# A Hymba layer on one core: weights of the heads, the GLU and the output projection split by two DMAs of GpSimd's queue

## The chip, the cores and the metric

The kernel runs on one core of a Trainium2 chip. The metric is the device time of one execution in microseconds; the time of a kernel is the median of its runs. The core has five engines that each run their own list of instructions in a fixed order: TensorE (PE), VectorE (DVE), ScalarE (ACT), GpSimd (POOL) and SyncE (SP, which here only issues DMAs). They wait for each other by semaphores.

## The reference

One layer of a hybrid decoder for one sequence of 1024 positions, width 1024, all in float32. Cut to what matters:

```
h = rms(x, norm1_w) * (1 + sc1) + sh1
u, q, k, v = split(h @ w_in, [512, 1024, 1152])        # "heads": q, k, v
y_ssm  = s5(u, ...)                                     # scan over positions, then
         # z = gelu(y);  out = z * sigmoid(z @ w_glu + b_glu)
y_attn = window_attention(rms(q), rms(k), v, rel_bias, sinks)   # window of 128
x = x + g1 * (concat(rms(y_ssm), rms(y_attn)) @ w_out)
h2 = rms(x, norm2_w) * (1 + sc2) + sh2
x = x + g2 * conv_ffn(h2, w_up, conv_w, conv_b, w_down)         # d_ff = 2816
```

sh1, sc1, g1, sh2, sc2, g2 come from `silu(c) @ w_mod + b_mod`.

## The kernel before

The kernel keeps the products near float32 by splitting each operand into two arrays of the type fp32r, a rounded half hi and the rest lo = array - hi. `mm3` (L143 to L147) then makes one product of three matmuls, hi by hi, hi by lo and lo by hi. So each weight has to be there twice before its lo can be used. `split` (L137 to L141) makes the pair from an array that stands in SBUF: ScalarE casts it into hi (L133), and VectorE, or GpSimd where the caller says so, subtracts hi from it into lo (L118).

The stages, with their place in the profiled execution:

- up to 128 us: modulation, first norm, operands of the S5 scan and its convolutions; the first two heads begin.
- 128 to 224 us: the six heads t0 to t5 (v, k and four pairs of q). `head_w` (L459) brings the weights of one head, 128 by 1024: a DMA of SyncE into the staging tile W0 (L461), a split into U0/U1 for even t and U2/U3 for odd t, and sixteen small matmuls that make a bias row. One head is 48 matmuls of 512 columns. VectorE does the scan, the norms of q and k and their splits beside it.
- 224 to 324 us: GELU (L725), the GLU and the first units of attention. The GLU weights go through W0 as two arrays and are split in four halves of 512 columns into HA and HB (L748 to L754). Attention runs in 16 units: ScalarE makes the exponentials (L835, L837), and a multiplication by the reciprocal of the sum (the rule PM picks GpSimd for it in all but two units) precedes PE's transposes and the product with v.
- 324 to 401 us: the rest of attention and the S5 half of the output projection. Its weights come in four arrays through W0 into HA and HB in turn (L897 to L901). VectorE makes the later modulation values from arrays that SyncE loads into S16 (`emit_mod`, L178).
- 401 to 477 us: the attention half of the output projection. `wload` (L869) brings eight arrays through W0 (W1 and W0 in turn for the last four) into pairs of U tiles.
- 477 us to the end: the conv FFN, up and down. Its weights have splits of their own that the change doesn't touch.

The order of the instructions on each engine is set ahead of the run: a scheduler with a simulated time line (L1358) gives each engine one list, and a tile name such as W0 or U0 is a slot whose next user waits until the last reader of the one before is done. A DMA that waits for its slot stands at the head of its engine's list, and what is behind it on that engine waits too. Before the change GpSimd issues no DMA in these stages; its list there holds only the multiplications of attention.

Of the kernel before, what the change touches and what calls it, by code (L numbers as in the profile page):

```python
# [9 lines left out]
F32 = mybir.dt.float32  # L10
# [4 lines left out]
ADD, SUB, MUL, MAX, MIN = ALU.add, ALU.subtract, ALU.mult, ALU.max, ALU.min  # L15
# [47 lines left out]
def hymba_kernel(ctx, tc, xT, c, wmod, wu, wkvq, small, consts, relb, pq, wglu, wout, wup, wdn, out):  # L63
# [7 lines left out]
    def new(tag, dt=F32):  # L71
        return pool.tile([128, SIZES.get(tag, 1024)], dt, tag=tag, name="t" + tag)
# [11 lines left out]
    def newr(tag):  # L84
        return RT(new(tag, F32R))

    vec, act, pol, sync = nc.vector, nc.scalar, nc.gpsimd, nc.sync
# [29 lines left out]
    def tt(eng, o, a, b, op):  # L117
        return eng.tensor_tensor(out=o, in0=a, in1=b, op=op)  # L118
# [12 lines left out]
    def cpy(e, o, i):  # L131
        if e == "a":
            act.copy(o, i)  # L133
        else:
            ENG[e].tensor_copy(out=o, in_=i)

    def split(x, src, hi_eng="a", lo_eng="v"):  # L137

        hi, lo = x
        cpy(hi_eng, hi.r, src)  # L140
        tt(ENG[lo_eng], lo.r, src, hi.f, SUB)  # L141

    def mm3(o, a, b, start, stop, chain=False):  # L143

        pe.matmul(o, a[0].r, b[0].r, start=start, stop=False, skip_group_check=chain)
        pe.matmul(o, a[0].r, b[1].r, start=False, stop=False, skip_group_check=chain)
        pe.matmul(o, a[1].r, b[0].r, start=False, stop=stop, skip_group_check=chain)  # L147
# [81 lines left out]
    for k in range(8):  # L229
        if k < 2:  # L230
            t_ = newr(("HA", "HB")[k])
# [6 lines left out]
    wst = None  # L238
    for k in range(8):
# [3 lines left out]
        if k % 2 == 0:  # L243
            wst = new(("W0", "A10")[k // 2 % 2])
            sync.dma_start(out=wst, in_=wu[k // 2])
        w = half(newr(f"U{k}") if k < 4 else wux[:, (k - 4) * 1024:(k - 3) * 1024])
# [27 lines left out]
    U = new("S16")[:, 0:4096]  # L274
# [182 lines left out]
    brow = pool.tile([2, 128 * 2], F32, name="brow")  # L457

    def head_w(t):  # L459
        wst = new("W0")  # L460
        sync.dma_start(out=wst, in_=wkvq[t])  # L461
        w = (newr(f"U{2 * (t % 2)}"), newr(f"U{2 * (t % 2) + 1}"))
        split(w, wst)
        if t >= 2:
            qn.append(new(("W1", "U4", "U5")[t - 2]) if t < 5 else qx)
        b, b2, r = abank(), abank(), brow[:, (t % 2) * 128:(t % 2 + 1) * 128]
        for k in range(8):
            ks = slice(k * 128, k * 128 + 128)
            pe.matmul(b[0:2, 0:128], shs[:, 2 * k:2 * k + 2], w[0].r[:, ks], start=(k == 0), stop=False)
            pe.matmul(b[0:2, 0:128], shs[:, 2 * k:2 * k + 2], w[1].r[:, ks], start=False, stop=(k == 7))  # L470
        vec.tensor_copy(out=r, in_=b[0:2, 0:128])
        with pe.pin(False):
            pe.matmul(b2[:, 0:1], r, ones[0:2, 0:1], start=True, stop=True)
        vec.tensor_copy(out=bcol[:, t:t + 1], in_=b2[:, 0:1])
        return w
# [145 lines left out]
    for q in range(4):  # L621
        sync.dma_start(out=kd[:, 8 * q:8 * q + 8, 112:240],
                       in_=ka[32 * q:32 * q + 16, :].rearrange("p (g x) -> p g x", x=128))
# [60 lines left out]
    for h in range(2):  # L684
        for i in range(4):
            q_ = newr(f"H{8 + 4 * h + i}")
            for kv in range(2):
# [3 lines left out]
                src = qn[i][p0, h * 512:h * 512 + 512]  # L691
# [23 lines left out]
    for i in range(8):  # L715
        b = bank[int(pick("YB", i))]
        for q in range(4):
            g = 4 * i + q
            o = b[:, q * 128:(q + 1) * 128]
            st = (SI if g % 2 else SR)[:, g // 2, 0:128]  # L720
# [7 lines left out]
    for m in range(4):  # L728
        zv = zT[m].rearrange("p (c t) -> p t c", t=8)
        for q2 in range(2):  # L730
            b = sbank()
            for q in range(4):
                t_ = 4 * q2 + q
# [13 lines left out]
    wg = []  # L747
    wgt = (newr("HA"), newr("HB"))  # L748
    for k in range(4):
        if k % 2 == 0:  # L750
            wst = new("W0")
            sync.dma_start(out=wst, in_=wglu[k // 2])
        wg.append(half(wgt[k // 2][:, (k % 2) * 1024:(k % 2 + 1) * 1024]))
        split(wg[k], wst[:, (k % 2) * 512:(k % 2) * 512 + 512])  # L754
    mx = {}
    bw = pool.tile([128, 8], F32, name="bw")
    ts(bw[:, 0:4], S("ons"), -0.5, MUL)
# [5 lines left out]
    for h in range(2):  # L763
# [9 lines left out]
        for n in range(4):  # L773
            src = zT[n][:, hs]
# [6 lines left out]
        for n in range(4):  # L781
            src = zT[n][:, hs]
# [27 lines left out]
    for n in range(8):  # L810
        av = bank[2]
        for kv in range(2):
# [6 lines left out]
            for i2 in range(2):  # L819
# [6 lines left out]
                for i1 in range(2):  # L826
                    i = 2 * i2 + i1
                    vec.tensor_tensor_reduce(  # L828
                        out=P[:, i, :], in0=b[:, i1 * 256:i1 * 256 + w_], in1=Tb[kv][:, i, 256 - w_:256],
# [31 lines left out]
    x = [xq[:, k * 1024:(k + 1) * 1024] for k in range(4)] + [new(f"X{k}") for k in range(4, 8)]  # L861
# [1 line left out]
        sync.dma_start(out=x[k], in_=xT[k])  # L863
    ld = [0]

    slots = [("U0", "U1"), ("U4", "U5"), ("U0", "U1")]
    slots += [(("U4", "U5"), ("U2", "U3"), ("U0", "U1"))[i % 3] for i in range(5)]

    def wload(src):  # L869
        i = ld[0]  # L870
        ld[0] += 1
        st = new("W0" if i < 4 else f"W{i % 2}")
        sync.dma_start(out=(st if len(src.shape) == 2 else st.rearrange("p (d c) -> p d c", d=2)), in_=src)
        w = (newr(slots[i][0]), newr(slots[i][1]))
        split(w, st)
        return w

    n2s = pool.tile([128, 8], F32, name="n2s")
# [1 line left out]
    wo2 = wout.rearrange("d p (b c) -> b p d c", b=2)  # L880
# [13 lines left out]
    wS = {}  # L894
    for i, d in enumerate(order):
        if i % 2 == 0:
            st = new("W0")  # L897
            sync.dma_start(out=st.rearrange("p (d c) -> p d c", d=2), in_=wo2[0, :, d:d + 2])
            t_ = newr(("HA", "HB")[(i // 2 + 1) % 2])
            w = (t_[:, 0:1024], t_[:, 1024:2048])  # L900
            split(w, st)  # L901
        wS[d] = w
        for h in range(2 if d > 3 else 1):
            proj(d, h, 0, bank[5 + h], w)
        for q in (2 * i, 2 * i + 1):
            with tc.issue_after(unit[MOD_AT[q]]):
                emit_mod(24 + q, mst[q % 3], cact3)
# [202 lines left out]
    G, W = {}, {}  # L1110
# [110 lines left out]
    for s_, (c_, i, p) in enumerate(steps):  # L1221
# [10 lines left out]
        if s_ in XP:  # L1232
            k = XP[s_]
# [128 lines left out]
```

## Time and profile before

| | us |
|---|---|
| median of 3 runs | 1139.48 |
| lowest and highest | 1139.41, 1142.07 |
| the profiled execution, its own time | 1142.15 |
| span of its trace | 1140.3 |

The own time of the profiled execution is 1.85 us longer than the span that the trace covers, from the first to the last instruction, and 2.67 us longer than the median of the runs. The mean clock that TensorE was granted is 0.958 of full speed. Engines are read by their busy time in a stage; what sets the end of a stage is read from the chain of waits, which follows the last instruction back to whatever released it.

### The profile page before, as it was taken

What the parts mean: (1) busy time and instruction counts of PE and PEld (TensorE: products, weight loads), DVE (VectorE), ACT (ScalarE), POOL (GpSimd) and SP (SyncE); (2) the same over time, 40 slices, a digit from 0 to 9 for tenths busy, and PEclk for the clock granted to TensorE, in tenths of its full rate; (3) what the DMA queues carried; (4) which work ended last, traced back from release to release, by engine and by line L of the source; (5) the groups of instructions that cost most, each with busy time, mean ns of one, the idle gap of its engine ahead of it and who ended that gap; (6) DMA issues with size and microseconds to landing.
All of it is one profiled execution on the core that took longest, in us unless ns stands there. A gap on an engine that the chain in (4) does not pass through costs nothing.

```text
span 1140.3 us, 13281 instructions
## 1 busy us (share of the span) xinstructions
PE 1053.4 (92%) x4692; PEld 828.2 (73%) x4692; DVE 957.5 (84%) x1541; ACT 550.2 (48%) x936; POOL 256.7 (23%) x137
## 2 busy tenths in 40 slices
PE   6979999688989899779999999999999989989998
PEld 4868777475646577657888888888888768768876
DVE  8996899969988988888777878797777787997985
ACT  5412443583874346745554545455444554434342
POOL 0000000002121001762122223212212142353541
PEclk9979999679989899989999999999999989999999
DMA  9501516025024743222223232423123359120002
GB/s 371 214 19 39 127 40 93 1 88 190 19 94 183 240 147 112 93 92 93 93 78 113 87 130 93 151 90 112 56 93 126 115 217 384 63 93 1 1 37 111
DMA packets 47333, 128.13 MB, mean 112 GB/s; under 512 B 6017, under 2 KB 13985, under 8 KB 47266
## 3 DMA queue, kind: packets, MB, share of 16 engines
q1 hardware_dynamic: 47266, 127.28, 32.8%
q8 instruction: 37, 0.61, 0.2%
q14 instruction: 30, 0.25, 0.1%
HBM read 105.28 MB, written 21.99 MB: 112 GB/s over the span
## 4 chain that ended last, share of the span: by engine, by line
PE 60%; DVE 29%; ACT 4%; DMA 3%; issue 3%; POOL 1%; SPq 0%; ACTq 0%; DVEq 0%; POOLq 0%
PE bk L97 54%; PE bk L99 6%; DVE tA L118 5%; DVE tU L118 3%; DVE tH L118 3%; DVE tS L118 2%; DVE tX L127 2%; DMA tW<-in_dram 2%; DVE bk L118 2%; DVE tS L180 1%; DVE tXQ L118 1%; DVE tXQ L127 1%; DVE tX L118 1%; DVE tX L180 1%; ACT tU L133 1%
## 5 line engine op out<-in xcount | busy, mean ns | idle before, releaser
L97 PE MATMUL bk<-tU,tU 128*128 128x512 f32 x516 | 124.9, 395 | 4.8 <-DVE tXQ L127 2.4
L97 PE MATMUL bk<-tA,tU 128*128 128x512 f32 x516 | 128.1, 395 | 0.8 <-DVE tA L118 0.8
L97 PEld LDWEIGHTS bk<-tU,tU 128*128 128x128 f32 x516 | 97.6, 190 | 27.8 <-issue 2.8
L97 PE MATMUL bk<-tH,tU 128*128 128x512 f32 x477 | 116.0, 392 | 0.0
L97 PEld LDWEIGHTS bk<-tA,tU 128*128 128x128 f32 x516 | 96.7, 188 | 24.2 <-DVE tA L118 1.4
L127 DVE SCALAR_TENSOR_TENSOR tX<-tH,sm,tX 128x1023 f32<-128x1023 f32 x66 | 100.5, 1523 | 8.0 <-ACT tX L1097 7.9
L97 PEld LDWEIGHTS bk<-tH,tU 128*128 128x128 f32 x477 | 89.1, 188 | 19.3
L97 PE MATMUL bk<-tA,tXQ 128*128 128x512 f32 x300 | 76.0, 401 | 2.1 <-ACT tH L1050 2.1
L118 POOL TENSOR_TENSOR tU<-tW,tU 128x512 fp32r<-128x512 f32 x25 | 36.3, 1462 | 174.1 <-ACT tU L133 152.4
L97 PE MATMUL bk<-tH,tA 128*128 128x512 f32 (+1 forms) x168 | 63.9, 509 | 11.4 <-ACT tH L133 7.6
L133 ACT CAST tU<-tW 128x512 fp32r<-128x512 f32 (+1 forms) x67 | 47.1, 710 | 48.9 <-PE bk L97 18.2
L97 PEld LDWEIGHTS bk<-tA,tXQ 128*128 128x128 f32 x300 | 57.4, 191 | 16.0 <-ACT tH L1050 2.5
L99 PE MATMUL bk<-tH,tU 128*128 128x512 f32 x267 | 64.0, 395 | 1.8 <-DVE tU L118 1.7
L118 POOL TENSOR_TENSOR tH<-tH,att 128x1024 f32<-128x1024 f32 (+1 forms) x9 | 19.1, 2124 | 195.8 <-DVE att L840 161.7
L118 DVE TENSOR_TENSOR tX<-tX,tX 128x512 f32<-128x512 f32 (+1 forms) x63 | 61.6, 981 | 0.8
L118 POOL TENSOR_TENSOR tXQ<-tW,tXQ 128x512 fp32r<-128x512 f32 x12 | 49.1, 4102 | 53.1 <-ACT tXQ L133 37.8
L99 PEld LDWEIGHTS bk<-tH,tU 128*128 128x128 f32 x267 | 49.6, 189 | 15.6 <-DVE tU L118 2.7
L97 PE MATMUL bk<-tXQ,tH 128*128 128x256 f32 (+2 forms) x224 | 51.9, 374 | 4.3 <-DVE att L828 4.3
L118 DVE TENSOR_TENSOR tU<-tW,tU 128x512 fp32r<-128x512 f32 (+2 forms) x43 | 37.8, 881 | 20.4 <-ACT tU L133 20.4
L97 PEld LDWEIGHTS bk<-tXQ,tH 128*128 128x128 f32 x224 | 45.1, 268 | 13.3 <-DVE att L828 9.0
L118 POOL TENSOR_TENSOR tU<-tX,tU 128x512 fp32r<-128x512 f32 x19 | 33.2, 1747 | 84.9 <-ACT tU L133 70.8
L118 DVE TENSOR_TENSOR tU<-tX,tU 128x512 fp32r<-128x512 f32 x39 | 31.3, 808 | 23.6 <-ACT tU L133 23.6
(349 smaller groups left out, 2398.9 us busy)
## 6 DMA issues: line engine op xcount, KB each, us to landing
tX<-in_dram SPq DMA_DIRECT2D x51, 512.0 KB, 3.3
tW<-in_dram SPq DMA_DIRECT2D x49, 512.0 KB, 3.3
tS<-in_dram SPq DMA_DIRECT2D x30, 512.0 KB, 6.0
gd<-tX SPq DMA_DIRECT2D x22, 512.0 KB, 2.9
tA<-in_dram SPq DMA_DIRECT2D x12, 512.0 KB, 9.7
tH<-in_dram SPq DMA_DIRECT2D x12, 512.0 KB, 4.2
tH<-gd SPq DMA_DIRECT2D x8, 512.0 KB, 4.7
tA<-gd SPq DMA_DIRECT2D x8, 512.0 KB, 8.9
```

Source lines behind the costliest of these rows:

```text
L97: return f(*a, **k)
L99: i = f(*a, **k)
L118: return eng.tensor_tensor(out=o, in0=a, in1=b, op=op)
L127: return vec.scalar_tensor_tensor(out=o, in0=a, scalar=s, in1=b, op0=op0, op1=op1)
L133: act.copy(o, i)
L180: vec.tensor_tensor_reduce(out=st, in0=st, in1=ca, scale=1.0, scalar=S("b_mod", j, 1), op0=MUL, op1=ADD, accum_out=mod[:, j:j + 1],)
```

## The change

A new helper `dsplit` takes the place of a staging load and a `split` where weights of the heads, the GLU and both halves of the output projection are brought in, 22 times in all. It issues a DMA on GpSimd's queue that reads the array from HBM and casts it into hi. ScalarE multiplies hi by -1 into lo. A second DMA on GpSimd's queue reads the array from HBM again and adds it onto lo. The staging tile W0 falls away there, and so do 20 loads on SyncE's queue and 22 subtractions on VectorE; 22 casts on ScalarE become 22 multiplications of the same width. GpSimd issues 44 DMAs that it did not issue before, 36 of 512 KB and 8 of 256 KB. The eight pairs of `wload` get other slots, among them W0/W1 for the third.

```diff
--- before.py
+++ after.py
@@ -139,6 +139,13 @@
         hi, lo = x
         cpy(hi_eng, hi.r, src)
         tt(ENG[lo_eng], lo.r, src, hi.f, SUB)
+
+    def dsplit(x, src, shape=None):
+
+        v = [(t_.r if shape is None else shape(t_.r)) for t_ in x]
+        pol.dma_start(out=v[0], in_=src)
+        act.mul(v[1], v[0].bitcast(F32), -1.0)
+        pol.dma_start(out=v[1], in_=src, accum_op=ADD)
 
     def mm3(o, a, b, start, stop, chain=False):
 
@@ -457,10 +464,8 @@
     brow = pool.tile([2, 128 * 2], F32, name="brow")
 
     def head_w(t):
-        wst = new("W0")
-        sync.dma_start(out=wst, in_=wkvq[t])
         w = (newr(f"U{2 * (t % 2)}"), newr(f"U{2 * (t % 2) + 1}"))
-        split(w, wst)
+        dsplit(w, wkvq[t])
         if t >= 2:
             qn.append(new(("W1", "U4", "U5")[t - 2]) if t < 5 else qx)
         b, b2, r = abank(), abank(), brow[:, (t % 2) * 128:(t % 2 + 1) * 128]
@@ -747,11 +752,8 @@
     wg = []
     wgt = (newr("HA"), newr("HB"))
     for k in range(4):
-        if k % 2 == 0:
-            wst = new("W0")
-            sync.dma_start(out=wst, in_=wglu[k // 2])
         wg.append(half(wgt[k // 2][:, (k % 2) * 1024:(k % 2 + 1) * 1024]))
-        split(wg[k], wst[:, (k % 2) * 512:(k % 2) * 512 + 512])
+        dsplit(wg[k], wglu[k // 2][:, (k % 2) * 512:(k % 2) * 512 + 512])
     mx = {}
     bw = pool.tile([128, 8], F32, name="bw")
     ts(bw[:, 0:4], S("ons"), -0.5, MUL)
@@ -863,16 +865,16 @@
         sync.dma_start(out=x[k], in_=xT[k])
     ld = [0]
 
-    slots = [("U0", "U1"), ("U4", "U5"), ("U0", "U1")]
-    slots += [(("U4", "U5"), ("U2", "U3"), ("U0", "U1"))[i % 3] for i in range(5)]
+    slots = [(f"U{i}", f"U{i + 1}") if i < 6 else ("W0", "W1") for i in (0, 4, 6, 2, 0, 4, 2, 4)]
+
+    def pairs(t_):
+        return t_.rearrange("p (d c) -> p d c", d=2)
 
     def wload(src):
         i = ld[0]
         ld[0] += 1
-        st = new("W0" if i < 4 else f"W{i % 2}")
-        sync.dma_start(out=(st if len(src.shape) == 2 else st.rearrange("p (d c) -> p d c", d=2)), in_=src)
         w = (newr(slots[i][0]), newr(slots[i][1]))
-        split(w, st)
+        dsplit(w, src, pairs)
         return w
 
     n2s = pool.tile([128, 8], F32, name="n2s")
@@ -894,11 +896,9 @@
     wS = {}
     for i, d in enumerate(order):
         if i % 2 == 0:
-            st = new("W0")
-            sync.dma_start(out=st.rearrange("p (d c) -> p d c", d=2), in_=wo2[0, :, d:d + 2])
             t_ = newr(("HA", "HB")[(i // 2 + 1) % 2])
             w = (t_[:, 0:1024], t_[:, 1024:2048])
-            split(w, st)
+            dsplit(w, wo2[0, :, d:d + 2], pairs)
         wS[d] = w
         for h in range(2 if d > 3 else 1):
             proj(d, h, 0, bank[5 + h], w)
```

The new order on each engine differs from the old one at the following places.

PE where head t1's first half ends and t2 begins (tHA, tHB, tH: the activations' halves; tU0/tU1: hi and lo of t2's weights; shs: the shift that makes the bias row). Before:

```order
L97 MATMUL bk0_63<-tH14_97,tU3_978 128x512
L97 MATMUL bk2_65<-tHA_85,tU0_1064 128x512 x2
L97 MATMUL bk3_66<-tHA_85,tU0_1064 128x512
L97 MATMUL bk6_69<-tX4_601,cn_73 128x512
L97 MATMUL bk3_66<-tHA_85,tU0_1064 128x512
L97 MATMUL bk2_65<-tHA_85,tU1_1065 128x512
L97 MATMUL bk5_68<-cn_73,brow_609 128x1
```

And after, on the same engine at the same place:

```order
L97 MATMUL bk0_63<-tH14_97,tU3_975 128x512
L97 MATMUL bk5_68<-cn_73,brow_609 128x1
L97 MATMUL bk6_69<-tX4_601,cn_73 128x512
L97 MATMUL bk2_65<-tHA_85,tU0_1060 128x512 x2
L97 MATMUL bk3_66<-tHA_85,tU0_1060 128x512 x2
L97 MATMUL bk5_68<-tU0_1060,shs_458 2x128
L97 MATMUL bk5_68<-tU1_1061,shs_458 2x128
```

In both, four matmuls of t2 can run on hi alone; what needs lo comes right behind them, and in the new order that is the bias row.

ACT at the end of the GELUs (the table loads switch ScalarE's function; L725 is the GELU, L835 and L837 the exponentials of attention). Before:

```order
L725 ACTIVATE tX7_1632<-bk6_69 128x4x8x16
L835 ACT_TABLE_LOAD
L835 ACTIVATE att_1992<-att_1992 128x4
L837 ACTIVATE tH4_1993,att_1992<-tH4_1993,att_1992 128x128 x4
L835 ACTIVATE att_1992<-att_1992 128x4
L837 ACTIVATE tH5_2023,att_1992<-tH5_2023,att_1992 128x128 x4
L133 CAST tHB_1797<-tW0_1804 128x512
L725 ACT_TABLE_LOAD
L725 ACTIVATE tX7_1632<-bk5_68 128x4x8x16
L133 CAST tHB_1797<-tW0_1804 128x512
L835 ACT_TABLE_LOAD
```

And after, where the GELU has L730 and the exponentials L837 and L839, and L147 is the negation in `dsplit`:

```order
L147 ACTIVATE tHA_1790<-tHA_1790 128x512
L730 ACTIVATE tX6_1625<-bk6_69 128x4x8x16
L730 ACTIVATE tX7_1626<-bk5_68 128x4x8x16
L730 ACTIVATE tX7_1626<-bk6_69 128x4x8x16
L837 ACT_TABLE_LOAD
L837 ACTIVATE att_1986<-att_1986 128x4
L839 ACTIVATE tH4_1987,att_1986<-tH4_1987,att_1986 128x128 x4
```

The last GELU now stands ahead of the exponentials, and one switch back and forth, two table loads, is gone.

POOL in the second half of attention (TENSOR_TENSOR: a unit's multiplication; L146 the casting DMA, L148 the adding one; tHA: weights of the S5 half of the output projection, tU: of the attention half). Before:

```order
L118 TENSOR_TENSOR tH_2381<-tH_2381,att 128x1024
L118 TENSOR_TENSOR tA_2417<-tA_2417,att 128x1024
L118 TENSOR_TENSOR tH_2491<-tH_2491,att 128x1024
L118 TENSOR_TENSOR tA_2529<-tA_2529,att 128x1024
L118 TENSOR_TENSOR tH_2565<-tH_2565,att 128x1024
```

And after, from the DMAs ahead of the multiplication that was the third of these:

```order
L146 DMA tU_2924<-in_dram 128x2x512
L146 DMA tHA<-in_dram 128x2x512
L118 TENSOR_TENSOR tH_2485<-tH_2485,att 128x1024
L148 DMA tU_2925<-in_dram 128x2x512
L148 DMA tHA<-in_dram 128x2x512
L118 TENSOR_TENSOR tA_2523<-tA_2523,att 128x1024
L146 DMA tU_3111<-in_dram 128x2x512
L118 TENSOR_TENSOR tH_2559<-tH_2559,att 128x1024
```

Each of the last three multiplications now has DMAs ahead of it that wait for a slot or for ScalarE's negation.

## Rows read from the trace of the kernel before

**Rows 1.** The page, its line of engines: busy time, share, instructions.
```profile
PE 1053.4 (92%) x4692; PEld 828.2 (73%) x4692; DVE 957.5 (84%) x1541; ACT 550.2 (48%) x936; POOL 256.7 (23%) x137
```

**Rows 2.** Busy time by stage: stretch, length, engines, clock, DMA share, GB/s.
```profile
128.00:224.00 96.00, 82.46 (x435) 61.55 (x423) 92.74 (x182) 41.74 (x63) 0.00 (x0) 0.92 0.32 64
256.00:324.00 68.00, 57.47 (x256) 38.37 (x256) 62.55 (x161) 44.55 (x114) 15.78 (x8) 0.93 0.29 99
324.00:369.00 45.00, 44.72 (x187) 28.28 (x186) 38.12 (x93) 24.26 (x70) 9.37 (x4) 0.95 0.46 163
369.00:401.00 32.00, 26.61 (x99) 17.16 (x98) 29.27 (x50) 11.26 (x17) 2.76 (x1) 0.89 0.70 229
515.00:1140.00 625.00, 605.15 (x2585) 488.56 (x2583) 509.37 (x607) 292.84 (x449) 180.51 (x106) 0.99 0.29 106
```

**Rows 3.** Chain of waits, 105 to 324 us: start, length, what.
```profile
105.53 17.63 PE bk L99 x181
...
138.13 1.13 DVE tU L118
...
173.64 1.22 DVE tU L118
...
201.69 0.70 DVE tU L118
...
245.05 1.28 ACT L725
...
247.47 1.28 ACT L835
...
308.36 1.14 DVE tHB L118
...
309.53 3.37 DMA tW<-in_dram
```

**Rows 4.** Chain of waits, 374 to 436 us.
```profile
374.42 1.15 DVE tHA L118
375.58 4.67 DMA tW<-in_dram
...
382.61 5.38 DMA tW<-in_dram
...
389.09 1.23 DVE tU L118
...
401.77 34.13 PE bk L99 x146
```

**Rows 5.** Time line of ACT in the heads: start, length, instruction, idle before it.
```profile
89.30 1.05 ACT L133 CAST tU<-tW 128x1024 fp32r<-128x1024 f32 x1
...
140.30 0.62 ACT L504 CAST tXQ<-tX 64x512 fp32r<-64x512 f32 x1
```

**Rows 6.** Time line of PE in the heads, and at the end of attention.
```profile
93.96 1.12 PE L99 MATMUL bk<-tU,shs 128*2 128x128 f32 x16
...
130.37 4.26 PE L99 MATMUL bk<-tH,tU 128*128 128x512 f32 x18
...
142.09 1.03 PE L97 MATMUL bk<-tHA,tU 128*128 128x512 f32 x2
...
195.15 3.26 PE L97 MATMUL bk<-tH,tU 128*128 128x512 f32 x13
...
387.79 2.95 PE L97 MATMUL bk<-tA,tHA 128*128 128x512 f32 x12
395.98 4.85 PE L97 MATMUL bk<-tA,tHA 128*128 128x512 f32 x12 [5.24 <-DVE tXQ L127]
```

**Rows 7.** DMA issues, whole span, then 360 to 400 us: KB, median us to landing.
```profile
tW<-in_dram SPq DMA_DIRECT2D x49, 512.0 KB, 3.3
...
tW<-in_dram SPq DMA_DIRECT2D x4, 512.0 KB, 4.7
```

**Rows 8.** POOL: the time line at 469 us, and line L118 by tile (ns).
```profile
469.29 31.15 POOL L118 TENSOR_TENSOR tXQ<-tW,tXQ 128x512 fp32r<-128x512 f32 x1 [5.30 <-ACT tXQ L133]
...
L118 POOL TENSOR_TENSOR tH<-tH,att x9: 1039/2161/2902, 243.5 to 370.6; 128x1024 f32<-128x1024 f32 x7, 128x512 f32<-128x512 f32 x2
```

## The prediction

> **What bounds the kernel now.** I read the busy times first. PE is busy for 92% of the span and DVE for 84%, GpSimd for 23% [rows 1], so time can only be won where PE waits. The busy times by stage say where that is. From 515 us on, PE is busy 605 of 625 us; the change edits nothing there, and I count it as zero. From 324 to 369 us PE is busy 44.72 of 45.00. From 128 to 224 us DVE is the fuller engine, 92.74 of 96 against PE's 82.46, and from 369 to 401 us PE has only 26.61 of 32 while DVE has 29.27 [rows 2]. The chain of waits was read next, for the pieces that belong to the weights. In the heads four of DVE's subtractions lie on it, 138.13 the first and 173.64 the last, of 1.10 to 1.22 us each, 4.57 together. Around 245 us two of ScalarE's table loads are on it, 1.28 each, and at 308 us one subtraction with the staging load behind it, 1.14 and 3.37 [rows 3]. From 374.42 to 390.32 us the chain is nothing but the staging tile W0 going round: subtract, load (4.67), cast, subtract, load (5.38), cast, subtract (1.23) [rows 4]. PE runs out of work behind it: it is idle for 5.24 us before 395.98, and the next 12 matmuls take 4.85 us where the 12 before took 2.95 [rows 6]. PE's busy rows from 401.77 on (34.13 us in one piece, rows 4) show it full again.
>
> **What a new pair costs.** Call D the time from the slot's release to the landing of lo. It holds a casting load, a negation and an adding load. No row shows a DMA that GpSimd issues, nor one that casts or adds. The nearest is SyncE's staging load of the same 512 KB, 3.3 us to landing at the median and 4.7 where the queue is busy [rows 7]. The negation is as wide as the cast that it replaces, 1.05 us [rows 5]. From below D is 3.3 + 1.05 + 3.3 = 7.65 us. From above I let the adding load cost two, since it also reads its destination, at the busy price: 4.7 + 1.05 + 9.4 = 15.2 us. I take 9.5, nearer the lower end, because the bytes and the array are those of the staging load; of it some 3.9 is the casting load, and about 4.5 is left for the adding one. Before, the staging tile hid the load, and cast and subtraction took only 1.05 + 1.22 after the slot was free. So a pair whose slot is freed late now comes later by about 7 us, and one whose slot is free early costs nothing on the path.
>
> **Heads: plus 4 us.** t0: ScalarE wrote the first half of the pair at 89.30 [rows 5], so the slot was free then; lo lands at 89.3 + 9.5 = 98.8. PE takes it for the bias row at 93.96 [rows 6]. That is 4.8 us of waiting, 3.0 to 10.5 by the bounds, on an engine on which the chain lies here (17.63 us in one piece from 105.53, rows 3); some 0.8 of it lies where PE waited for the bias row anyway, so plus 4. t1 is wanted only behind t0's last matmuls, at 134.6, and costs nothing. t2: its slot is freed when t0's last matmuls end, 130.37 + 4.26 = 134.6. The casting load lands at 138.5, but ScalarE is in its casts of k until 140.30 + 0.62 = 140.9, so the negation ends at 142.0 and lo lands at 146.5. PE arrives at 142.09 and can run four matmuls on hi, to 143.0: a wait of 3.5 us (0 to 9). t3 to t5 are freed early enough at a D of 9.5. DVE in turn loses its four subtractions, minus 4.57 on the chain. Both can't be had: PE's last head matmuls end at 195.15 + 3.26 = 198.4 [rows 6] and DVE takes their result at 201.69 [rows 3], 3.3 us later. With PE 3.5 later that margin is used up, and DVE, 4.57 faster, waits for PE. I count zero for this second step (from -4.6 to +5), and +4 for the heads.
>
> **GELU and GLU: minus 2 us.** The last GELU moves ahead of the exponentials, so that one switch back and forth falls away, 2 x 1.28 = 2.56 us [rows 3]. The first exponentials start later by about one GELU, which takes back some of it. The GLU weights are wanted only after the first units of attention. Bounds -2.6 and 0.
>
> **First half of the output projection, 256 to 324 us: minus 2 us.** Gone from the chain are 1.14 and 3.37 at 308.36 [rows 3]; that is 4.5, and DVE, 62.55 of 68 us busy [rows 2], stays next. But GpSimd's list now has the four DMAs of two pairs ahead of the multiplication of a unit. That one takes 2.16 us [rows 8] and used to start as soon as DVE was done; now it can wait for a slot and for ScalarE. I take half back. Bounds -4 and +3.
>
> **End of attention, 369 to 401 us: minus 6 us.** W0 no longer goes round: the first pairs of the attention half have slots of their own, the third (W0/W1) is loaded long before. Also three subtractions leave DVE. The most that PE can win is its idle 5.24 and the 1.9 by which 4.85 exceeds 2.95, 7.1 together [rows 6]. What is late next is DVE's modulation work, which fills the 29.27 us; less three subtractions it is 25.6, under PE's 26.6. Against it: the last three multiplications of attention stand behind DMAs, and PE has no slack from 324 to 369 us. I take 6, bounds -7 and 0.
>
> **Nothing for the rest.** The later pairs of `wload` (401 to 477 us) are hidden beside a full PE; uncovered, each would cost up to D less its lead. SyncE's 20 loads less win nothing, no chain piece waits for its issue. The second reading of some 10 MB lies beside a DMA share of at most 0.70 [rows 2], and is a part of D's upper bound.
>
> **Sum.** +4 - 2 - 2 - 6 = -6 us. The profiled execution took 1142.15 us (its span 1140.3 and 1.85 around it), so it would take 1136.15. That execution lay 2.67 us over the median of the runs, 1139.48, and the changed kernel is compared with that: 1139.48 - 6 = 1133.5 us. A difference under 0.3%, 3.4 us, can't be told from no change here.
>
> **Rivals.** *First, slower: GpSimd writes its DMAs late.* A GpSimd subtraction took 31.15 us at 469.29, where the larger multiplications of attention take 2.2 at the median, while DVE ran one subtraction after the other [rows 8]; GpSimd got nowhere until DVE let go. In the heads DVE is as full (92.74 of 96). If that, or a slow adding load, brings D to 15, t0 costs 9.7 instead of 4 and t2's wait grows to 9, of which 5.7 shows beyond the margin; t4 and t5, which would now come late too, add 2 more by my estimate; attention gives back the 2 at 256 us and half of the 6. That is 9.7 + 5.7 + 2 - 2 + 0 - 3 = +12.4, so 1152 us. It decides from a D of about 12, where t0 and t2 have eaten the 6 us. Against it: in the heads DVE does short operations with gaps, and the row stands alone: the longest of the nine multiplications in attention took 2.9 us, beside a DVE that was busy for 62.55 of 68 us [rows 2, 8].
>
> The Trainium skill ("SBUF — State Buffer", the box on the trap that DVE blocks DMA, and the lines on the shared port pair) speaks against the change: descriptors of DMAs from GpSimd's queue are written by GpSimd, and an operation of DVE that holds both ports keeps it from writing them; it gives 620 ns alone and about 3100 ns beside a copy. By it, an estimate, two DMAs of a pair would each come 2.5 us later, D would be 14.5, and the time that of this rival. The same page says that a DVE operation with two inputs in SBUF blocks only what GpSimd reads, which would spare most of the heads, where DVE multiplies and adds.
>
> *Second, no change: the won time is lost to the order on GpSimd's list.* The last multiplications wait behind two adding DMAs that themselves wait for ScalarE; one such wait of 5 us in the stage where PE has 0.28 us of slack takes back what 369 to 401 us give. +4 - 2 - 2 - 6 + 5 = -1, 1138.5 us. For it: each engine's list is fixed. Against it: the multiplications have some lead over the transposes that use them.
>
> *Third, a larger gain.* If D is at its lower end, t0 costs 2, t2 nothing, and DVE's 4.57 come through: 2 - 4.6 - 2.5 - 3 - 7 = -15, 1124.5 us.
>
> **How the numbers follow.** The forecast, 1133.5 us, has 0.42; the larger gain 0.08; no change 0.20; the first rival 0.30, since D rests on rows of another queue. So faster by over 0.3% has 0.50, within 0.3% 0.20, slower 0.30. The range leaves out the upper part of the third rival's gain and of the first rival's loss: 1125 to 1152 us. For the forecast alone it is 1128 to 1136.
>
> **What would show it.** The DMA rows of the changed kernel give D's two loads; PE's idle time before the bias row of t0 (near 94 us) and at t2 (near 143 us) shows 4 and 3.5 us if I am right, over 8 each if the first rival is. From 369 to 401 us PE's idle 5.24 should be gone; a wait of PE for a GpSimd multiplication between 330 and 380 us would be the second rival. ScalarE should show two table loads fewer around 245 us. The prediction fails if D is over 12 us, or if attention waits for GpSimd.

## The result: 3.25% slower

The changed kernel takes 1177.18 us at the median (1176.69 to 1179.41, 4 runs) where the kernel before, in the same session, takes 1140.31 (1139.41 to 1142.07, 4 runs): a ratio of 1.0325, interval 1.0306 to 1.0345. The forecast was 1133.5 and the range ended at 1152. The profiled execution of the changed kernel has a span of 1175.1 us, 34.8 more than the 1140.3 of before.

The engines' line of its page, to be held against [rows 1]: no engine but GpSimd has more to do than before, and DVE is busy for 19.5 us less. PE runs the same 4692 matmuls in 1059.3 us instead of 1053.4; the other 29 of the 35 us are idle time of PE.

```profile
PE 1059.3 (90%) x4692; PEld 832.7 (71%) x4692; DVE 938.0 (80%) x1519; ACT 549.1 (47%) x934; POOL 295.4 (25%) x181
```

Busy time by stage of the changed kernel (columns as in [rows 2]; stretches by the clock of each run, so work has moved between them):

```profile
128.00:224.00 96.00, 85.72 (x480) 65.49 (x477) 89.61 (x173) 38.69 (x57) 5.65 (x8) 0.92 0.47 88
...
369.00:401.00 32.00, 25.23 (x100) 15.34 (x100) 22.57 (x51) 12.09 (x35) 13.27 (x8) 0.89 1.00 301
401.00:477.00 76.00, 56.10 (x218) 42.75 (x216) 46.91 (x73) 28.07 (x44) 10.12 (x9) 0.87 0.51 144
...
515.00:1140.00 625.00, 598.02 (x2542) 482.14 (x2543) 521.77 (x632) 299.51 (x459) 198.36 (x104) 0.98 0.29 105
```

The kernel before, from 401 to 477 us:

```profile
401.00:477.00 76.00, 74.35 (x317) 59.14 (x316) 62.62 (x90) 46.97 (x75) 18.97 (x9) 1.00 0.36 126
```

PE is busy for 56 of 76 us from 401 to 477, where the kernel before kept it busy for 74; from 369 to 401 its share is no better than that in [rows 2], though DVE is now busy for 22.57 us instead of 29.27. The DMA share there is 1.00, where it was 0.70.

To place the loss I put the starts of PE's matmuls in order, of which both kernels have 4692, and took the difference for the n-th, counted from 0. The order of a few matmuls differs, so a single row can be off by some us; a step that stays is lost or won time.

```
matmul  before us   after   after_fix (see below)
   240     88.39    -0.08      -0.19
   280     94.92    +6.24      +6.34     head t0
   400    111.25    +7.77      +7.64
   720    150.27   +14.58     +14.37     head t2
   920    190.30   +13.87     +13.66
  1000    225.60    +4.03      +3.71     heads done
  1360    304.94    +5.87      +5.53
  1640    379.12    +4.70      +5.13     end of attention
  1720    406.39    +9.30      +9.30
  1760    415.46   +28.90      +9.75     attention half of the output projection
  1920    454.51   +37.21     +15.10
  2160    531.38   +34.73     +13.81     FFN
  4260   1036.19   +34.43     +14.59
```

The heads lose 14 us and give 10 back. The end of attention loses 5 instead of winning 6. The attention half of the output projection, for which the prediction has zero, loses 28, of which 2.5 come back by the FFN, which is untouched.

PE's time line of the changed kernel, the rows with idle time before them at these places (start, length, instruction, idle and what ended it):

```profile
95.39 0.70 PE L97 MATMUL bk<-tHA,tU 128*128 128x512 f32 x2 [1.29 <-DMA tU<-in_dram]
99.81 1.76 PE L99 MATMUL bk<-tU,shs 128*2 128x128 f32 x15 [3.72 <-DMA tU<-in_dram]
...
153.03 0.22 PE L97 MATMUL bk<-tU,shs 128*2 128x128 f32 x1 [1.88 <-DVE bcol L479]
155.46 1.76 PE L97 MATMUL bk<-tU,shs 128*2 128x128 f32 x15 [2.20 <-DMA tU<-in_dram]
...
433.14 1.19 PE L99 MATMUL bk<-tH,tU 128*128 128x512 f32 x2 [10.53 <-DMA tU<-in_dram]
440.04 7.21 PE L99 MATMUL bk<-tH,tU 128*128 128x512 f32 x22 [5.71 <-DMA tU<-in_dram]
...
476.94 0.70 PE L99 MATMUL bk<-tH,tU 128*128 128x512 f32 x2 [1.27 <-DMA tU<-in_dram]
483.94 6.33 PE L99 MATMUL bk<-tH,tU 128*128 128x512 f32 x17 [6.30 <-DMA tU<-in_dram]
```

Each pair of rows is one new pair of weights. At t0, at 433 and at 477 us PE first waits for hi, runs what it can on hi alone, two matmuls or a few more, and waits again for lo: 5.0, 16.2 and 7.6 us in all. At t2 hi is there in time; PE waits 1.9 us for DVE's copy of a bias column, runs one short matmul and waits 2.2 us for lo, 4.1 in all.

GpSimd's time line of the changed kernel shows why (L146 casts into hi, L148 adds onto lo; the idle time before a row ends with the release of the slot or with the negation):

```profile
89.50 0.57 POOL L146 DMA_DIRECT2D tU<-in_dram  x1 [59.71 <-PE bk L99]
...
94.48 0.89 POOL L148 DMA_DIRECT2D tU<-in_dram  x1 [3.07 <-ACT tU L147]
...
142.47 0.55 POOL L146 DMA_DIRECT2D tU<-in_dram  x1 [22.62 <-PE bk L99]
...
428.62 0.74 POOL L146 DMA_DIRECT2D tU<-in_dram  x1 [5.35 <-DVE tH L127]
434.38 1.19 POOL L148 DMA_DIRECT2D tU<-in_dram  x1 [5.03 <-ACT tU L147]
...
470.31 0.77 POOL L146 DMA_DIRECT2D tU<-in_dram  x1 [1.22 <-PE bk L99]
```

At t0 the slot is free at 89.5 and lo has landed at 99.8: 10.3 us from release to lo, in three legs that the chain of waits of the changed kernel names one by one:

```profile
89.50 3.53 DMA tU<-in_dram
...
93.11 1.07 ACT tU L147
...
94.48 5.29 DMA tU<-in_dram
```

At 428.62 it is the fourth pair of the attention half. The change gave it U2/U3, and that slot is released by DVE's L127, part of the norm of the second half of the positions, which itself comes right before PE wants the pair. PE has stood since 422.6, and from 428.62 to 440.04 it has two matmuls to do. The last pair's slot, U4/U5, is released by PE at 470.3, and PE stands waiting for hi from 475.7 on and for lo until 483.94. From release to lo it is 12.9 us at t2, 11.4 at 428 us and 13.6 at the last pair.

### The profile page after: what moved, and what is told of

Read it like the earlier page. It is cut to its first block, busy times and chain, and to the rows that moved or that the text cites. A ratio compares the mean times of both kernels' runs of the same rounds, so it can differ in the third digit from the quotient of the medians.

```text
span 1175.1 us, 13324 instructions
## 1 busy us (share of the span) xinstructions
PE 1059.3 (90%) x4692; PEld 832.7 (71%) x4692; DVE 938.0 (80%) x1519; ACT 549.1 (47%) x934; POOL 295.4 (25%) x181
## 4 chain that ended last, share of the span: by engine, by line
PE 58%; DVE 21%; issue 11%; DMA 5%; ACT 4%; POOL 1%; SPq 0%; POOLq 0%; DVEq 0%; ACTq 0%
PE bk L97 54%; DVE tA L118 4%; PE bk L99 3%; DVE tH L118 3%; DVE tU L118 3%; DMA tU<-in_dram 2%; DMA tS<-in_dram 2%; DVE tX L127 1%; DVE tS L187 1%; DVE tX L118 1%; DVE tXQ L118 1%; DVE tH L127 1%; DVE tXQ L127 1%; DVE tS L118 1%; DMA tX<-in_dram 1%
## 5 line engine op out<-in xcount | busy, mean ns | idle before, releaser
L97 PE MATMUL bk<-tH,tU 128*128 128x512 f32 x477 | 117.8, 395 | 0.0
L127 DVE SCALAR_TENSOR_TENSOR tX<-tH,sm,tX 128x1023 f32<-128x1023 f32 x66 | 100.2, 1519 | 7.2 <-ACT tX L1097 6.9
L99 PE MATMUL bk<-tH,tU 128*128 128x512 f32 x243 | 67.0, 433 | 28.4 <-DMA tU<-in_dram 23.8
L97 PE MATMUL bk<-tH,tA 128*128 128x512 f32 (+1 forms) x168 | 61.5, 492 | 9.2 <-ACT tH L133 5.6
L118 POOL TENSOR_TENSOR tU<-tW,tU 128x512 fp32r<-128x512 f32 x25 | 37.1, 1491 | 118.1 <-ACT tU L133 103.1
L118 POOL TENSOR_TENSOR tXQ<-tW,tXQ 128x512 fp32r<-128x512 f32 x12 | 49.9, 4162 | 52.3 <-ACT tXQ L133 32.5
L118 DVE TENSOR_TENSOR tX<-tX,tX 128x512 f32<-128x512 f32 (+1 forms) x63 | 61.6, 982 | 1.5 <-DMA tX<-in_dram 0.6
L118 POOL TENSOR_TENSOR tU<-tX,tU 128x512 fp32r<-128x512 f32 x19 | 32.9, 1735 | 85.4 <-ACT tU L133 71.3
L97 PE MATMUL bk<-tXQ,tH 128*128 128x256 f32 (+2 forms) x224 | 49.4, 360 | 4.8 <-DVE att L830 4.6
L127 DVE SCALAR_TENSOR_TENSOR tXQ<-bk,mod,tXQ 128x512 f32<-128x512 f32 x56 | 39.9, 742 | 15.1 <-PE bk L97 9.1
L118 DVE TENSOR_TENSOR tU<-tX,tU 128x512 fp32r<-128x512 f32 x39 | 31.4, 808 | 23.6 <-ACT tU L133 23.5
L97 PE MATMUL bk<-tH,tXQ 128*128 128x512 f32 x192 | 46.4, 391 | 0.0
L118 DVE TENSOR_TENSOR tA<-tA,tA 128x512 f32<-128x512 f32 (+3 forms) x45 | 40.5, 910 | 6.8 <-ACT tA L133 4.2
```

What stands on the lines that cost most here:

```text
L97: return f(*a, **k)
L99: i = f(*a, **k)
L127: return vec.scalar_tensor_tensor(out=o, in0=a, scalar=s, in1=b, op0=op0, op1=op1)
```

## Experiments

The theory after this look (A): a new pair costs where its slot is freed shortly before PE needs it, because from release to lo it takes some 10 to 14 us instead of a cast and a subtraction; where the slot is free early it costs nothing. Rivals: GpSimd's list holds up attention's multiplications (B), or each of the 44 DMAs costs something wherever it is (C).

### One part alone

Each kernel is the kernel before with `dsplit` at some of the four places only:

```diff
 def head_w(t):            # heads_only
-    wst = new("W0")
-    sync.dma_start(out=wst, in_=wkvq[t])
     w = (newr(f"U{2 * (t % 2)}"), newr(f"U{2 * (t % 2) + 1}"))
-    split(w, wst)
+    dsplit(w, wkvq[t])
 # wload_only: the hunks of the change at slots and wload alone
 # gluws_only: its hunks at wg and wS alone
 # no_wload:   all its hunks but those at slots and wload
```

**heads_only.** 

> Only the six weights of the heads are split by DMAs; GLU and output projection as before the change. Theory A (a pair costs where its slot is freed late and PE needs it at once; the trace of after lags 14 us behind before at t2 and only 6 us of it is left at 350 us): slower by 4 to 9 us, about 1146. Rival B (the queue of GpSimd in attention is what costs): no more than 2 us slower. Rival C (every dsplit costs alike, 37 us by 44 DMAs): 12 DMAs, 10 us slower.

Measured: 1146.22 us, ratio 1.0064 (1.0043 to 1.0086).

**wload_only.** 

> Only the eight weights of the attention half of the output projection are split by DMAs, in the slots of the changed kernel; the rest as before the change. Theory A: the later pairs wait for slots that PE or DVE free just ahead of their use, and cost about 12 us each time from release to lo; slower by 20 to 30 us, about 1165. Rival B: the multiplications of attention late, 5 to 10 us slower. Rival C: 16 DMAs, 13 us slower.

Measured: 1169.96 us, ratio 1.0267 (1.0248 to 1.0286).

**gluws_only.** 

> Only the GLU halves and the S5 half of the output projection are split by DMAs; heads and the attention half as before the change. Theory A: their slots are free early, so no loss: between 6 us faster and 1 us slower, about 1137. Rival B: GpSimd's multiplications stand behind these DMAs, 5 us or more slower. Rival C: 16 DMAs of which half are of 256 KB, 10 us slower.

Measured: 1143.0 us, ratio 1.0025 (1.0010 to 1.0039).

**no_wload.** 

> The changed kernel with the attention half of the output projection brought in as before the change (staging tile and old slots). Theory A: most of the 37 us goes with it; about 2 to 8 us slower than before, 1145. Rival B: still 12 us or more slower, since the multiplications of attention stay behind DMAs. Rival C: 28 DMAs, 23 us slower.

Measured: 1145.58 us, ratio 1.0050 (1.0031 to 1.0069).

The attention half alone makes 30.6 of the 37 us, just over the 20 to 30 of A, and without it 6 are left. That is A's order, and neither C's (13 and 23) nor B's, in which no_wload would stay at 12 or more. For the GLU and the S5 half A was not exact: no loss was expected beyond 1 us, and the runs lie 3.7 above before, between 1137.69 and 1144.62. The profiled execution was the fastest of them; in its trace PE is 9.7 us ahead at the 1440th matmul and 3.4 at the 2160th, and no wait for a DMA of `dsplit` stands out. What the slower ones lose, and where, no trace of mine shows.

### The slot, and the length

The next kernels change only the slots of the attention half: `w_fixslots` is wload_only with other slots, `w_newslots_split` the kernel before, staging and split included, with the slots of the change.

```diff
 # w_fixslots
-    ... for i in (0, 4, 6, 2, 0, 4, 2, 4)]
+    ... for i in (0, 4, 6, 0, 2, 4, 0, 2)]
 # w_newslots_split
-    slots = [("U0", "U1"), ("U4", "U5"), ("U0", "U1")]
-    slots += [(("U4", "U5"), ("U2", "U3"), ("U0", "U1"))[i % 3] for i in range(5)]
+    slots = [(f"U{i}", f"U{i + 1}") for i in (0, 4, 0, 2, 0, 4, 2, 4)]
```

**w_fixslots.** 

> As wload_only (1170), but the fourth pair takes U0/U1 instead of U2/U3 and the fifth and eighth take U2/U3, the seventh U0/U1. In wload_only PE stood 10.50 and 5.81 us at the fourth pair, whose slot U2/U3 is freed by DVE only after the norm of the second half. Theory A (slot freed late times the length of a dsplit, about 12 us): that wait shrinks to some 5 us since U0/U1 is freed 6 us ahead of use, and the last wait of 6.3 us goes; 1148 to 1153. Rival D (the pair's length costs in any slot): no more than 8 us better than wload_only, 1162 or more.

Measured: 1148.8 us, ratio 1.0082 (1.0065 to 1.0099).

**w_newslots_split.** 

> The kernel before, with staging and split, but the slots of the changed kernel for the pairs of the attention half (the third in U0/U1, as W0/W1 is the staging tile). Theory A: the fourth pair still waits for DVE to free U2/U3, but then only for a cast and a subtraction, 2.3 us instead of about 12: PE stands some 8 us there; 1146 to 1150. Rival E (the slots are harmless, the two DMAs alone cost 30 us): 1139.

Measured: 1143.28 us, ratio 1.0030 (1.0017 to 1.0043).

Four numbers in `slots` give back 21 of 31 us. The change's slots with staging and split (the third pair apart) cost only 4, less than A's 7 to 11: PE waits 2.74 us there, as the norm comes earlier in that order, so the slot is not freed at the same place. The slots cost 4 us with staging, the two DMAs 9 in the better slots, and both together 31: most of the loss is a late slot times a long fill. The same numbers in the whole changed kernel:

**after_fix.** 

> The changed kernel with the slots of w_fixslots, nothing else. Theory A (the slot of the fourth pair, and of the eighth, are most of the loss): 20 to 26 us of the 37 go, 1151 to 1157. Rival C (all dsplits cost alike): no more than 8 us go, 1169 or more.

Measured: 1156.07 us, ratio 1.0147 (1.0128 to 1.0166): 21 us of the 37 go. In the table above its column leaves that of after by 19 us at the 1760th matmul and by 3 more at the 1920th, where the fourth and the eighth pair stand. What stays, some 15 us by that column, is about 4 each in the heads and at the end of attention and 6 in the attention half.

### What a pair's length is made of

In the heads, three changes to the length or to where it is met:

```diff
 # heads_not02: t0 and t2 by staging and split as before, t1, t3, t4, t5 by dsplit
 # heads_cast, in head_w: hi by the casting DMA, lo as before the change
     wst = new("W0")
     sync.dma_start(out=wst, in_=wkvq[t])
+    pol.dma_start(out=w[0].r, in_=wkvq[t])
+    tt(vec, w[1].r, wst, w[0].f, SUB)
 # heads_noadd, in dsplit
-    pol.dma_start(out=v[1], in_=src, accum_op=ADD)
+    pol.dma_start(out=v[1], in_=src)
```

**heads_not02.** 

> Heads t1, t3, t4 and t5 split by DMAs, t0 and t2 by staging and split, the rest as before the change. Theory A: heads_only lost its time at t0 (6.6 us of lag) and t2 (another 6.6) alone; without them between 4 us faster and 1 us slower than before, 1138. Rival C (each dsplit costs alike): two thirds of the loss of heads_only stay, 1144.

Measured: 1143.3 us, ratio 1.0034 (1.0021 to 1.0048).

**heads_cast.** 

> All six weights of the heads: hi by a casting DMA of GpSimd's queue, lo by DVE's subtraction from the staging tile as before the change; ScalarE's cast, the negation and the adding DMA are left out. Theory A (what costs is the chain of two loads and a negation behind the release): from release to lo 3.5 + 1.2 instead of 10.3 us; PE waits about 1 us at t0 and none at t2; 1139 to 1142. Rival F (any DMA on GpSimd's queue comes late beside a busy DVE): as slow as heads_only, 1146.

Measured: 1142.58 us, ratio 1.0029 (1.0014 to 1.0045).

**heads_noadd.** 

> As heads_only, but the second DMA only casts and writes; it adds nothing (the lo halves of the heads' weights are then the rounded array instead of the rest, which this leaves wrong in the result; the rest is done in full). Theory A': the adding load costs more than the casting one because it reads its destination too; in after it took 5.3 us at t0 where the casting one took 3.5. Without adding it lands in 3.5 to 4, and the lag at t0 falls from 6.9 by 1.5 to 2 us. Rival (the second load is slower for another reason, such as GpSimd's writing of it): 5 us or more, lag unchanged.

Measured: 1140.99 us, ratio 1.0018 (1.0005 to 1.0031).

```
matmul  before us   heads_only  heads_not02  heads_cast  heads_noadd
   240     88.39       -0.87       +0.79       -1.49       -0.67
   400    111.25       +6.89       +5.03       +0.77       +4.58
   720    150.27      +13.47       +4.97       +1.18       +7.11
  1000    225.60       +2.81       -1.04       -2.14       -1.16
```

With the casting load and DVE's subtraction, about 5 us from release to lo, the steps at t0 and t2 are nearly gone, with the same number of casting DMAs beside a full DVE. So the steps come from the chain of two loads and a negation, not from GpSimd's queue as such. The total of heads_cast lies 3 us above before all the same, half a us outside the range; its lag is below zero at the 1000th matmul, so what it loses comes behind the heads, and no run shows why. In heads_not02 the step at t2 went, as expected, but another of 5 us came near t0: the scheduler now runs t1's matmuls there, and PE waits 2.65 us at 102.35 for t1's lo. The experiment moved the exposed pair instead of removing it. Its total missed A's range and is near C's 1144, but by its trace the loss near t0 is one exposed pair, so the total can't tell the two apart.

The landing times of the second DMA, the lines of the trace on the adding line of heads_only and, below it, of heads_noadd:

```profile
DMA to landing us min/median/max: 5.3/5.5/5.9
```

```profile
DMA to landing us min/median/max: 3.5/3.6/4.6
```

Adding makes a load of the same bytes 1.9 us longer. Without it the lag at t0 is 2.3 us smaller, and behind t2 6.4: there PE's wait for lo falls from 2.23 to 0.48 us, and the mean granted clock from 142 to 160 us is 1.00 instead of 0.81. By the totals, 5.7 of heads_only's 6.9 us hang on those 1.9.

### The gain that did not come at the end of attention

In w_fixslots no slot is late any more before 403 us, yet PE stands there longer than the 5.24 us of [rows 6]. ACT, DVE and PE of w_fixslots at that place, each row with the idle time before it:

```profile
397.53 1.06 ACT L147 ACTIVATE tU<-tU 128x1024 fp32r<-128x1024 f32 x1 [8.94 <-DMA tU<-in_dram]
...
399.14 0.69 DVE L118 TENSOR_TENSOR tH<-tH,tH 128x512 f32<-128x512 f32 x1 [8.76 <-ACT tH L1006]
...
403.70 7.13 PE L99 MATMUL bk<-tH,tU 128*128 128x512 f32 x24 [9.26 <-DVE tXQ L127]
```

ScalarE stands at a negation whose casting load is still under way, behind it waits a square for the next norm (L1006), DVE waits for that, and PE for DVE. ScalarE's list has become the queue. The test puts the negation elsewhere:

```diff
 # w_fix_negpool, in dsplit
-    act.mul(v[1], v[0].bitcast(F32), -1.0)
+    pol.tensor_scalar(out=v[1], in0=v[0].bitcast(F32), scalar1=-1.0, scalar2=None, op0=MUL)
 # w_negmix: that for the first four pairs, ScalarE for the later four
 # w_first4: that for the first four pairs, staging and split for the later four
 # gluws_fix_negpool: as w_fix_negpool, and the change's hunks at wg and wS
```

**w_fix_negpool.** 

> As w_fixslots (1149), but GpSimd instead of ScalarE multiplies hi by -1. In wload_only and w_fixslots PE stands 8.6 and 9.3 us for DVE ahead of the first matmuls of the attention half, DVE 8.1 and 8.8 us for ScalarE, and ScalarE 8.9 us in a negation whose casting load is under way. Theory G (the negation holds up ScalarE's list): these waits go to under 4 us, and the kernel comes to 1141 to 1146. Rival H (PE's wait there comes from the loads of the modulation values, late beside the weights' second reading): PE still stands 8 us or more, and the time stays within 2 us of 1149.

Measured: 1149.63 us, ratio 1.0086 (1.0069 to 1.0103).

**w_negmix.** 

> As w_fix_negpool (1150), but only the first four pairs are negated on GpSimd, the later four on ScalarE again. If the early gain and the late loss are separate (theory A and G): the gain of 4 us at 403 us stays, the later loss is that of w_fixslots, about 2 to 5 us instead of 14; 1138 to 1143. If the loss behind 403 us has another cause: 1147 or more.

Measured: 1138.93 us, ratio 0.9997 (0.9985 to 1.0010).

**w_first4.** 

> As w_negmix, but the later four pairs come by staging and split as before the change, in the slots of w_fixslots. Theory A and G: the gain of 4 us at 403 us stays and nothing is lost behind it, 1134 to 1138, faster than before and after. If the first four pairs take time from what follows (slots, DMA traffic, order): 1139 or more.

Measured: 1140.91 us, ratio 1.0018 (1.0007 to 1.0028).

**gluws_fix_negpool.** 

> A version meant to be faster: the heads as before the change, GLU and both halves of the output projection split by DMAs with the slots of w_fixslots and the negation on GpSimd. Theory A and G together (no pair with a late slot, nothing behind a negation on ScalarE): 1136 to 1143. Rival B (the multiplications of attention stand behind GpSimd's DMAs and negations): 1146 or more.

Measured: 1145.06 us, ratio 1.0045 (1.0028 to 1.0062).

```
matmul  before us   wload_only  w_fixslots  w_fix_negpool  w_negmix  w_first4
  1640    379.12       -2.23       -1.51       -1.30        -1.88     -4.26
  1720    406.39       +3.39       +3.82       -3.89        -4.46     -6.86
  1760    415.46      +23.23       +4.28       -3.43        -4.00     -6.40
  1920    454.51      +32.64       +6.36      +11.08        -2.08     -1.89
  2160    531.38      +29.93       +6.44      +10.02        -2.74     -2.47
```

The total of w_fix_negpool speaks for the rival, 1149.63 against 1148.8; its trace speaks for G. With the negation on GpSimd PE's wait falls from 9.26 to 3.10 us, and the gain that the prediction looked for is there, 4 us at the 1720th matmul. It is lost later, because GpSimd takes three times as long to negate, and the later pairs are longer by it. PE and GpSimd of w_fix_negpool:

```profile
395.75 7.36 PE L99 MATMUL bk<-tH,tU 128*128 128x512 f32 x24 [3.10 <-DVE tXQ L127]
432.11 8.17 PE L99 MATMUL bk<-tH,tU 128*128 128x512 f32 x24 [4.55 <-DMA tU<-in_dram]
```

```profile
392.42 3.13 POOL L147 TENSOR_SCALAR tU<-tU 128x1024 fp32r<-128x1024 f32 x1 [7.10 <-DMA tU<-in_dram]
```

w_negmix decides it: the early negations on GpSimd, the late ones on ScalarE, and the early gain is there, while of the late loss of 15 us between the 1720th and the 1920th matmul 2.4 are left. The two are separate, as G and A have it. In the profiled executions w_negmix and w_first4 end 2 to 3 us ahead of before, but by their runs they are no faster: 0.9997 and 1.0018. w_first4, meant to be the faster version, missed its 1134 to 1138 and came out where its rival has it, 1139 or more; gluws_fix_negpool missed its 1136 to 1143. In the trace of w_first4 most of the lead is gone between the 1760th and the 1920th matmul, where PE has caught up with DVE and waits for squares that go into the next norm:

```profile
420.26 1.55 PE L99 MATMUL bk<-tH,cn 128*128 128x512 f32 x2 [2.71 <-DVE tH L118]
```

Whether the first four pairs have a part in that wait no run shows. No version that I ran beats the kernel before.

## Where the prediction was right and where it failed

**What a pair costs: within the bounds, and too small.** D was taken as 9.5 us, with bounds 7.65 and 15.2. At t0 it is 10.3 (3.5, 1.1 and 5.3), at 428 us 11.4, and 12.9 at t2 and 13.6 at the last pair, over the 12 that the prediction names as a sign of failing. The adding load is 5.5 us where I had 4.5; the casting load of the last pair took 6.5 where I had 3.9.

**Heads: the sum was right by luck, two errors that cancel.** t0's wait was 5.0 us for 4.8 predicted; at t2 lo was late by about as much as predicted, 4.1 for 3.5, if the wait for the bias column before it is counted in. But the waits cost more than their idle time: the lag goes from 6.24 at the 280th matmul to 7.77 at the 400th, while PE has work all the time. From 100 to 120 us, in the kernel before and then in the changed one:

```profile
100.00:120.00 20.00, 20.00 (x182) 16.41 (x181) 10.22 (x27) 5.37 (x10) 0.32 (x2) 1.00 0.36 74
```

```profile
100.00:120.00 20.00, 20.00 (x138) 16.78 (x137) 6.35 (x17) 5.29 (x10) 0.32 (x2) 0.84 0.10 20
```

PE is busy all 20 us in both, but at a mean granted clock of 0.84 instead of 1.00, so partly at the lower of its two levels after its wait. Behind t2's wait the clock is 0.85 from 157 to 170 us. So the lag reaches 14 us on 9.1 us of waiting. Then 10 come back by the 1000th matmul, where I had counted DVE's 4.57 as lost to PE; what the 10 are made of no run separates. What is left is +4.0, the number predicted.

**GELU and the first half of the projection: -4 predicted, +0.7 measured.** From the 1000th to the 1640th matmul the lag stays near 4 to 7 us and ends where it began, within the bounds. ScalarE has 12 table loads instead of 14, as forecast. With the heads as before the change (gluws_only) the lag falls by 3.8 us between the same two matmuls; why it does not in the changed kernel no run shows.

**End of attention: wrong, -6 predicted, +4.6 measured** (from +4.70 to +9.30). The step that failed is "What is late next is DVE's modulation work, which fills the 29.27 us; less three subtractions it is 25.6, under PE's 26.6". It weighed busy times and left out what DVE waits for. DVE's busy time did fall, to 22.57 us, and PE still stands 5.00 us for it, 5.24 before [rows 6], and 2.39 once more behind the attention. ScalarE, DVE and PE of the changed kernel there, and two loads from its chain of waits:

```profile
374.39 1.06 ACT L147 ACTIVATE tU<-tU 128x1024 fp32r<-128x1024 f32 x1 [3.63 <-DMA tU<-in_dram]
375.62 1.06 ACT L147 ACTIVATE tHA<-tHA 128x1024 fp32r<-128x1024 f32 x1 [0.17 <-DMA tHA<-in_dram]
376.58 0.49 ACT L839 ACTIVATE tA<-tA,att 128x256 f32<-128x256 f32 x1
...
378.77 0.16 DVE L118 TENSOR_TENSOR att<-att 128x4 f32<-128x4 f32 x1 [4.28 <-ACT tA L839]
...
388.89 1.28 DVE L187 CUSTOM_DVE_ANT_0 tS<-tS,sm 128x1024 f32<-128x1024 f32 x1 [1.90 <-DMA tS<-in_dram]
...
392.56 4.82 PE L97 MATMUL bk<-tA,tHB 128*128 128x512 f32 x12 [5.00 <-DVE tXQ L127]
...
408.94 7.37 PE L99 MATMUL bk<-tH,tU 128*128 128x512 f32 x24 [2.39 <-DVE tXQ L127]
```

```profile
369.39 6.21 DMA tHA<-in_dram
...
383.19 5.67 DMA tS<-in_dram
```

DVE stands 4.28 us for a unit's exponentials (L839), which come behind two negations on ScalarE, and these behind their casting loads. Then it stands 1.90 us for a modulation array (S16), whose load takes 5.67 us. The clause that the second reading lies beside a DMA share of at most 0.70 failed with it: the share is 1.00 from 369 to 401 us. No run separates the two in the changed kernel. In w_fixslots it was ScalarE's list, as w_fix_negpool shows: I moved the casts into negations one for one and did not ask what the negation waits for. Before, a cast waited there for its load too, 4.1 us at the longest; in w_fixslots the negation waits 8.94 us, for a load that starts only when the slot is free, and all that stands behind it on ScalarE waits too. What takes the gain away in the changed kernel comes with the pairs of `wload`: without them, in no_wload, the lag falls by 6.6 us between the same two matmuls, the gain that I had predicted.

I had looked for such a queue on GpSimd's list, the second rival. There it is harmless: PE waits 2.2 us in all for these multiplications, 3.3 before. One of them does stand behind an adding DMA that waits 10.98 us for ScalarE's negation, but PE is full there and does not need it yet. GpSimd's time line of the changed kernel, and what PE waited for from GpSimd's multiplications into tH in the whole span (us, times, longest):

```profile
336.41 1.20 POOL L148 DMA_DIRECT2D tW<-in_dram  x1 [10.98 <-ACT tW L147]
337.19 2.35 POOL L118 TENSOR_TENSOR tH<-tH,att 128x1024 f32<-128x1024 f32 x1
```

```profile
PE bk L97 <- POOL tH L118: 2.2, 2, 1.5
```

**The rest: wrong, 0 predicted, +28 measured by the 1920th matmul** (+25 by the end). The step that failed is "The later pairs of wload are hidden beside a full PE". For the heads I asked for each pair when its slot is freed and when PE wants it; here I did not, although the diff changes the slots. The clause "uncovered, each would cost up to D less its lead" had no pair put to it. It fits the last one, 7.6 us of a D of 13.6, but is too low for the fourth: 16.2 us at a D of 11.4, because PE already stood for 6.0 us when the slot was freed. 21 of the 37 us lie in the four numbers that w_fixslots and after_fix change.

**The rivals.** The first had the right sign and the wrong place. D passed the 12 us from which it was to decide at t2 and at the last pair, but the largest loss lies behind the heads and hangs on a slot, and nothing in the trace shows GpSimd late in writing its DMAs. Its DMA instructions, the casting and the adding ones of the changed kernel (ns, min, median, max):

```profile
L146 POOL DMA_DIRECT2D tU<-in_dram x13: 541/740/1202, 89.5 to 470.3; - x13
```

```profile
L148 POOL DMA_DIRECT2D tU<-in_dram x13: 852/1182/1216, 94.5 to 478.2; - x13
```

The longest of these took 1.2 us, with DVE busy for 89.61 of 96 us in the heads. The Trainium skill ("SBUF — State Buffer", the box on the trap that DVE blocks DMA and the section behind it) warns of descriptors that GpSimd cannot write while DVE holds both ports, 620 ns turning into about 3100. In the heads nothing points to a delay of that size: without adding, a load of GpSimd's queue landed in 3.6 us at the median in the heads, near the 3.3 of SyncE's [rows 7]. Of DVE's 173 instructions from 128 to 224 us 151 have two inputs, and for these the same page has GpSimd blocked at most where it reads.

## What to carry to other kernels

A staging tile that looks like a needless copy is also a prefetch: it separates the load from the release of the slot. When loads go straight into the slots, ask of every slot when it is freed and by whom, and when its next pair is wanted; the whole fill, here 10 to 14 us, lies between the two. And when an operation keeps its engine and length but gets another releaser, look at what stands behind it on that engine.

## What the runs showed of the hardware that I had not expected

A DMA that adds onto its destination in SBUF took 5.5 us to land at the median where the same load without adding took 3.6 (512 KB, heads_only and heads_noadd), and GpSimd needs longer to issue it, 0.87 us against 0.53 in those two traces. GpSimd negates 128 by 1024 in 2.8 to 3.8 us where ScalarE takes 1.06. And a wait of PE of 5 us was followed by 20 us of unbroken work at a mean granted clock of 0.84, which cost another 1.5 us.
